# MLP operands made without the norm's factor, and weight sums made in DRAM, in an encoder block on one core

## The chip, the cores and the metric

One of the eight cores of a Trainium2 chip. The metric is the device time of one execution in microseconds (us): the time before is the median of three runs, 1359.18 us (1358.5 to 1359.72). The engines are PE (matrix products), DVE, ACT and POOL (elementwise work), SP (DMA queues), as the profile names them; POOL and ACT have DMA queues too.

## The reference

One layer over 1024 positions of width 1024, all in fp32:

```python
h = rmsnorm(x, norm_mix_g)
z = h @ w_in                                   # split into xc, bg, cg and latents
y_conv = bg * dwconv_centred(cg * xc, conv_w)  # width 512, 3 positions
y_mla = mla_attention(...)                     # 8 heads, from the latents
x = x + concat([y_conv, y_mla]) @ w_o
hf = rmsnorm(x, norm_ffn_g)                    # x * rsqrt(mean(x*x) + eps) * g
a = dwconv_centred(hf @ w_up, ffn_conv_w, ffn_conv_b)
g, u = split(a, 2)                             # 2 x 2816
x = x + (silu(g) * u) @ w_down
gate = sigmoid(rmsnorm(x, ple_norm_g) @ w_ple_gate)
x = x + gate * (p @ w_ple_proj)
return rmsnorm(x, final_norm_g)
```

The norm's factor is one number for each position, a column of the kernel's transposed layout. So it can be multiplied on a product's result as well as on its operand; the gain, one number for each channel, can't.

## The kernel before

Activations lie transposed, channels on the 128 partitions and 1024 positions along the free side, so x is eight tiles (chunks) of 128 x 1024. Each fp32 product is made of three reduced-precision products of high and low parts: an operand is copied to its high part (ACT, `put`, `load_unit`) and the rest is subtracted into the low part (DVE or POOL); `gemm` then issues high by high, high by low and low by high for every 512 columns.

In order of time: latents, conv heads (four of three products each, 60 to 190 us), values, attention (245 to 467; PE, DVE, ACT and POOL share the softmax, and `values(j)` closes each pair of query blocks with POOL's cast and difference, L554 and L555), the attention's half of the output projection (`out_mla`, 474 to 523), the norm of the MLP with the embeds (`embed(d)`, eight products of the layer's input embedding), and the MLP's up projection from 544 to 996, the down projection, the gate and the final norm.

The up projection uses seven products of 512 x 512 blocks in place of eight for each of 22 chunks of the inner width (a `Unit`, steps 1 to 7). The moving operands are four blocks and four sums of blocks of the normed x; the stationary ones are the weights' blocks a11, a12, a22 and sums s1 to s4, which DVE adds for each unit in `stationary` (L654 to L657) before they too are split:

```python
TERMS = {1: ("a11", "b11"), 2: ("a12", "b21"), 3: ("s4", "b22"), 4: ("a22", "t4"),
         5: ("s1", "t1"), 6: ("s2", "t2"), 7: ("s3", "t3")}
```

`up_moving` makes the moving operands: `scaled` multiplies x, in place, by gain and norm factor (L723, 16 halves), `diff` (L726) makes the differences t1 to t4, `put` the high (L734, ACT) and low parts (L726, DVE). The norm's factor comes from two groups of small matmuls that are slipped between those of embeds 2 and 4: sums over the channels (L228) and, after `norm_root`, a broadcast to all partitions (L253). So nothing of `up_moving` can begin before embed 4. The first two units run as a pair, step by step, with embeds 6 and 7 behind step 1; all others run one after another with step 4 one unit late (`run`). Each product's result is read out of PSUM by ACT (a copy) or DVE (L790), goes through a three-point convolution (`conv3`: one ACT step, L261, two DVE steps, L262 and L263) and the silu, and the result is stored to `gud` in DRAM.

What sets the order: the program's order on each engine is made by a scheduler from costs, except where a stretch is put under a manual order, which the text itself then gives; DVE is so from the norm to the end of `up_moving`. A wait holds everything behind it on its engine. Pools of tiles free their memory when the last reader is done, and whatever is placed there waits for that.

Of the kernel before, what the change touches and what calls it, by code (L numbers as in the profile page):

```python
# [33 lines left out]
def tile_block(ctx, tc, xT, pT, wlat, wun, wdn, wuq, wukv, vecs, cst, out):  # L34
# [182 lines left out]
    def norm(sh, sl, dim):  # L217
        n = sh.shape[1] // P
# [185 lines left out]
    for b in range(4):  # L404
# [9 lines left out]
        tt(out=t1, in0=pb, in1=t1, op=ALU.mult)  # L414
# [225 lines left out]
    def stationary(g, u, n, mid, mk, later):  # L640
        lo, hi = slice(0, n), slice(n, 2 * n)
        a = {}

# [10 lines left out]
        tt(out=s14[:, lo], in0=u[:, lo], in1=u[:, hi], op=ALU.add)  # L654
        tt(out=s23[:, lo], in0=s14[:, lo], in1=g[:, lo], op=ALU.subtract)
        tt(out=s14[:, hi], in0=g[:, hi], in1=s23[:, lo], op=ALU.subtract)
        tt(out=s23[:, hi], in0=g[:, lo], in1=u[:, lo], op=ALU.subtract)  # L657
# [17 lines left out]
    class Unit:  # L675
# [3 lines left out]
        def step(self, i):  # L679
# [34 lines left out]
    def up_moving(rs, then):
        sub = ALU.subtract
        bs = [{} for _ in range(4)]
        low = [None]

        def scaled(c, i):
            o = x1[c][:, HALF[i]]
            stt(out=o, in0=o, scalar=vc(V_FFN + c), in1=rs[i], op0=ALU.mult, op1=ALU.mult)  # L723

        def diff(o, p, q):
            tt(out=o, in0=p, in1=q, op=sub)  # L726

        def behind(fn):
            if low[0]:
                low[0]()  # L730
            low[0] = fn

        def put(src, h, z):
            nc.scalar.copy(out=h, in_=src)  # L734
# [391 lines left out]
```

## Time and profile before

| | before |
|---|---|
| median of 3 runs | 1359.18 us |
| profiled execution | 1356.78 us, of which span 1355.0 |
| mean granted clock of PE | 0.989 |
| busy: PE, DVE, ACT, POOL | 1323.1, 1006.1, 597.3, 261.3 us |
| moved by DMA | 117.38 MB, 87 GB/s |
| conv heads | 60 to 190 us |
| attention | 245 to 467 us |
| output projection, embeds, norm | 474 to 544 us |
| up projection: first pair, the 20 others | 544 to 609, 609 to 999 us |

The profile is one execution; its span is the time from the first to the last instruction. In a row of a group stand line, engine, operation, tiles, shapes and count, then busy us, mean ns of one, idle time before them, and who ended it. In a row of a timeline stand start and length in us; idle time before it, with its releaser, is in brackets. A matmul's length runs past the start of the next one, so work of PE is counted from start to start.

### The profile page before, as it was taken

What the parts mean: (1) busy time and instruction counts of PE and PEld (TensorE: products, weight loads), DVE (VectorE), ACT (ScalarE), POOL (GpSimd) and SP (SyncE); (2) the same over time, 40 slices, a digit from 0 to 9 for tenths busy, and PEclk for the clock granted to TensorE, in tenths of its full rate; (3) what the DMA queues carried; (4) which work ended last, traced back from release to release, by engine and by line L of the source; (5) the groups of instructions that cost most, each with busy time, mean ns of one, the idle gap of its engine ahead of it and who ended that gap; (6) DMA issues with size and microseconds to landing.
All of it is one profiled execution on the core that took longest, in us unless ns stands there. A gap on an engine that the chain in (4) does not pass through costs nothing.

```text
span 1355.0 us, 16462 instructions
## 1 busy us (share of the span) xinstructions
PE 1323.1 (98%) x6354; PEld 1087.7 (80%) x6354; DVE 1006.1 (74%) x1336; ACT 597.3 (44%) x839; POOL 261.3 (19%) x222
## 2 busy tenths in 40 slices
PE   9999999999999999879999999999999999999997
PEld 7877788888888887658888888888877888888897
DVE  7478923799999957988887888888665555557786
ACT  5323422788888834543443444344331111125433
POOL 0286452455555510000000000000010000000000
PEclk9999999999999999979999999999999999999998
DMA  6201134200000254203222222222174222121123
GB/s 215 78 31 47 47 133 148 78 1 17 1 17 1 68 212 171 94 16 124 78 78 78 94 78 78 78 94 74 66 292 165 95 94 94 55 78 55 49 83 111
DMA packets 38894, 117.38 MB, mean 87 GB/s; under 512 B 4256, under 2 KB 9632, under 8 KB 38816
## 3 DMA queue, kind: packets, MB, share of 16 engines
q1 hardware_dynamic: 35824, 107.30, 22.7%
q10 hardware_dynamic: 1840, 4.83, 0.9%
q0 software_dynamic: 1152, 4.19, 0.8%
q8 instruction: 50, 0.82, 0.3%
q14 instruction: 28, 0.23, 0.0%
HBM read 88.00 MB, written 28.31 MB: 86 GB/s over the span
## 4 chain that ended last, share of the span: by engine, by line
PE 85%; DVE 9%; issue 2%; POOL 2%; ACT 1%; DMA 0%; POOLq 0%; SPq 0%; ACTq 0%
PE bk L139 56%; PE big L139 9%; PE small L139 4%; PE small L534 4%; PE small L547 2%; PE big L504 2%; PE big L508 2%; PE big L506 2%; PE small L546 2%; DVE tmp L163 1%; DVE xt L726 1%; DVE tmp L263 1%; DVE tmp L262 1%; DVE b L726 1%; DVE rbc L164 1%
## 5 line engine op out<-in xcount | busy, mean ns | idle before, releaser
L139 PE MATMUL bk<-gu,whi 128*128 128x512 f32 x704 | 194.7, 398 | 2.8 <-DVE x L904 2.2
L139 PE MATMUL bk<-b,wm 128*128 128x512 f32 x792 | 192.8, 396 | 1.7 <-DVE b L726 1.4
L139 PEld LDWEIGHTS bk<-b,wm 128*128 128x128 f32 x792 | 148.5, 188 | 38.7 <-DVE b L726 2.5
L139 PEld LDWEIGHTS bk<-gu,whi 128*128 128x128 f32 x704 | 133.0, 189 | 36.0 <-issue 2.6
L904 DVE TENSOR_TENSOR x<-bk,x 128x512 f32<-128x512 f32 x112 | 71.9, 687 | 89.3 <-PE bk L139 88.8
L139 PE MATMUL bk<-xt,wm 128*128 128x512 f32 x528 | 129.3, 399 | 7.6 <-DVE xt L726 5.4
L128 ACT ACTIVATE whi<-wraw 128x1024 fp32r<-128x1024 f32 (+2 forms) x55 | 51.3, 933 | 187.7 <-PE bk L139 135.4
L139 PEld LDWEIGHTS bk<-xt,wm 128*128 128x128 f32 x528 | 100.8, 192 | 32.6 <-DVE xt L726 7.8
L139 PE MATMUL bk<-b,whi 128*128 128x512 f32 x352 | 112.4, 400 | 3.1 <-DVE b L726 3.1
L646 POOL TENSOR_TENSOR wm<-wraw,wm 128x512 fp32r<-128x512 f32 x22 | 28.8, 1311 | 448.9 <-ACT wm L645 448.9
L139 PE MATMUL bk<-gu,wlo 128*128 128x512 f32 x352 | 111.3, 397 | 0.0
L790 DVE TENSOR_TENSOR tmp<-bk,tmp 128x512 f32<-128x512 f32 x110 | 75.6, 687 | 30.6 <-PE bk L139 30.5
L521 POOL TENSOR_SCALAR tmp<-tmp,sm 128x256 f32<-128x256 f32 x64 | 70.2, 1097 | 101.2 <-DVE sm L514 98.5
L261 ACT ACTIVATE tmp<-tmp,vec 128x1024 f32<-128x1024 f32 x44 | 54.5, 1238 | 71.1 <-DVE tmp L790 71.1
L511 DVE TENSOR_REDUCE mx<-big 128x1 f32<-128x1024 f32 x64 | 78.0, 1218 | 10.3 <-PE big L508 9.8
L537 DVE TENSOR_TENSOR ptl<-small,pth 128x512 fp32r<-128x512 f32 x128 | 83.1, 679 | 1.2 <-ACT pth L536 0.9
L139 PEld LDWEIGHTS bk<-b,whi 128*128 128x128 f32 x352 | 66.9, 190 | 20.2 <-DVE b L726 4.2
L262 DVE SCALAR_TENSOR_TENSOR tmp<-tmp,vec 128x1023 f32<-128x1023 f32 x48 | 63.9, 1331 | 21.6 <-ACT tmp L261 19.2
L139 PEld LDWEIGHTS bk<-gu,wlo 128*128 128x128 f32 x352 | 66.4, 189 | 16.0
L536 ACT CAST pth<-small 128x512 fp32r<-128x512 f32 x128 | 69.0, 591 | 19.8 <-PE small L534 17.3
L513 ACT ACTIVATE tmp<-big,mx 128x1024 f32<-128x1024 f32 x64 | 72.1, 1127 | 5.2 <-DVE sm L514 2.6
L139 PE MATMUL big<-hh,whi 128*128 128x512 f32 x224 | 71.0, 397 | 3.3 <-DVE tmp L414 3.1
(291 smaller groups left out, 2793.6 us busy)
## 6 DMA issues: line engine op xcount, KB each, us to landing
wraw<-in_wun_dram SPq DMA_DIRECT2D x73, 512.0 KB, 3.2
gud<-tmp SPq DMA_DIRECT2D x22, 512.0 KB, 2.6
tmp<-gud SPq DMA_DIRECT2D x22, 512.0 KB, 4.3
wraw<-in_wdn_dram SPq DMA_DIRECT2D x24, 384.0 KB, 3.1
tmp<-in_xT_dram SPq DMA_DIRECT2D x15, 512.0 KB, 4.1
x1d<-tmp SPq DMA_DIRECT2D x8, 512.0 KB, 2.8
xt<-x1d SPq DMA_DIRECT2D x8, 512.0 KB, 6.4
x2d<-xt SPq DMA_DIRECT2D x8, 512.0 KB, 2.7
```

What stands on the lines that cost most here:

```text
L128: act(out=wh, in_=raw, func=AF.Copy)
L139: mm(p, w, x[:, s], start=a, stop=z, skip_group_check=more)
L261: act(out=t, in_=src, func=AF.Identity, scale=vc(w + 1), bias=vc(bias))
L262: stt(out=t[:, 1:S], in0=src[:, 0:S - 1], scalar=vc(w), in1=t[:, 1:S], op0=ALU.mult, op1=ALU.add)
L511: nc.vector.tensor_reduce(m, p, AX.X, ALU.max, negate=True)
L513: act(out=e, in_=p, func=AF.Exp, bias=m, accum_out=su)
L521: nc.gpsimd.tensor_scalar(out=e[:, w:S], in0=e[:, w:S], scalar1=su, scalar2=None, op0=ALU.mult)
L534: nc.tensor.transpose(t[:, k, :], e[:, (g * 4 + k) * P:(g * 4 + k) * P + P], ident)
L536: nc.scalar.copy(out=pth[:, ks, qs], in_=t)
L537: tt(out=ptl[:, ks, qs], in0=t, in1=f(pth)[:, ks, qs], op=ALU.subtract)
L790: add = lambda o, p, q: tt(out=o, in0=p, in1=q, op=ALU.add)
L904: tt(out=x1[d][:, s], in0=q, in1=x1[d][:, s], op=ALU.add)
```

## The change

1. *Moving operands without the norm's factor.* `gain(c)` (ACT, in place) multiplies a half of x by the gain alone once its half of x2 has been stored. Operands of chunks 0, 1 and 2 (b11, t1, t3: `put_1`, `put_3`) are made inside the loop of the output projection, from d = 4 on, and the others around the embeds. No `scaled` is left. The norm's factor is copied by ACT from PSUM to `rr`, and DVE multiplies it on the results: two halves of the gate (L858 in place of ACT's copy, L867) and the whole of the other (L871) in each unit. Signs change with it: b22 is negated, and so are the convolution weights of the neighbours.
2. *Weight sums in DRAM.* The up weights come as four block arrays. For each pair of chunks four plain DMAs (DRAM to DRAM, 512 KB) and four that add to their destination make s1 to s4 (`block_sums`, `add_blocks`), all on POOL's queue: 24 in attention, one behind each `values`, for the first three pairs of chunks, and 64 beside the MLP, four in each unit. A unit loads seven blocks of 256 KB instead of two of 512 KB.
3. *Order.* All eight embeds come ahead of the pair's first step (`embed(1)` has the norm's first matmuls in its middle, `embed(5)` its broadcast ahead of it); the pair's convolutions are put off to between its last steps, the third unit's weights are begun there. POOL has a manual order from attention to the MLP's end.
4. *Memory and smaller edits.* x1 lies in halves of 512 columns and is loaded and stored so; b21 and b22 lie where the attention's results did, which is kept up to the MLP's end; in the conv heads ACT copies a head's third product out of PSUM ahead of DVE's multiplication.

```diff
@@ norm @@
-                    tiny.append(lambda t=t, i=i, z=z: mm(p8[0][:, 2 * t:2 * t + 2], z[:, t * P:t * P + P], onesr[:, 0:2], start=i == 0, stop=i == 1))
+                    tiny.append(lambda t=t, i=i, z=z: mm(p8[0][:, 2 * t:2 * t + 2], z[t // 4][:, t % 4 * P:t % 4 * P + P], onesr[:, 0:2], start=i == 0, stop=i == 1))
@@ conv heads @@
-        tt(out=t1, in0=pb, in1=t1, op=ALU.mult)
+        bc = ft()
+        nc.scalar.copy(out=bc, in_=pb)
+        tt(out=t1, in0=bc, in1=t1, op=ALU.mult)
@@ attention @@
+    wsum = [{m: dram.tile([64, 2048], F32, name=f"w{m}_{b}") for m in ("s1", "s2", "s3", "s4")} for b in range(NFF // 2)]
+    dmas = []
+
+    def block_sums(bs):
+        for m, src, op in (("s1", A21, None), ("s2", A11, None), ("s3", A11, None), ("s4", A12, None),
+                           ("s1", A22, ALU.add), ("s3", A21, ALU.add), ("s2", "s1", ALU.add), ("s4", "s2", ALU.add)):
+            for b in bs:
+                dmas.append((wsum[b], m, src, b, op))
+
+    def add_blocks():
+        if dmas:
+            w, m, src, b, op = dmas.pop(0)
+            i = w[src] if isinstance(src, str) else wup[src, 64 * b:64 * b + 64]
+            if op is None:
+                nc.gpsimd.dma_start(out=w[m], in_=i)
+            else:
+                nc.gpsimd.dma_start(out=w[m], in_=i, accum_op=op, max_dma_last_dim=8192)
+
+    block_sums(range(3))
+    pool_order.enter_context(tc.manual_schedule(engines={mybir.EngineType.Pool}))
...
             values(i // 2 - 1)
+            add_blocks()
@@ output projection @@
+    def gain(c):
+        for x in x1[c]:
+            act(out=x, in_=x, func=AF.Copy, scale=vc(V_FFN + c))
...
     for d in range(NC_):
         out_mla(d, [3] if d < 3 else [0, 1, 2, 3])
         if d < 7:
-            for p, s in pieces(accs[d]):
-                tt(out=x1[d][:, s], in0=p, in1=x1[d][:, s], op=ALU.add)
-            square_acc(ss, x1[d], d == 0, nc.vector)
-        nc.sync.dma_start(out=x2d[d], in_=x1[d]) if d < 7 else None
+            q = ss if d == 0 else ft()
+            for p, x, s in zip(accs[d] if isinstance(accs[d], list) else halves(accs[d]), x1[d], HALF):
+                tt(out=x, in0=p, in1=x, op=ALU.add)
+                act(out=q[:, s], in_=x, func=AF.Square)
+                nc.sync.dma_start(out=x2d[d][:, s], in_=x)
+            if d:
+                tt(out=ss, in0=ss, in1=q, op=ALU.add)
+            gain(d)
+        if d in (4, 5, 6):
+            put_1(d - 4)
+            put_3(d - 4)
+            behind(None)
@@ stationary @@
-        tt(out=s14[:, lo], in0=u[:, lo], in1=u[:, hi], op=ALU.add)
-        tt(out=s23[:, lo], in0=s14[:, lo], in1=g[:, lo], op=ALU.subtract)
-        tt(out=s14[:, hi], in0=g[:, hi], in1=s23[:, lo], op=ALU.subtract)
-        tt(out=s23[:, hi], in0=g[:, lo], in1=u[:, lo], op=ALU.subtract)
@@ up_moving @@
-        def scaled(c, i):
-            o = x1[c][:, HALF[i]]
-            stt(out=o, in0=o, scalar=vc(V_FFN + c), in1=rs[i], op0=ALU.mult, op1=ALU.mult)
@@ up_unit @@
-        raws = [load_raw(wun[U_UP + 2 * c + j]) for j in range(2)]
+        load(g[:, T1S], block(wup[A11], c))
+        load(g[:, T2S], block(wup[A12], c))
+        load(u, block(wup[A22], c))
+        for to, m in ((s14[:, T1S], "s1"), (s14[:, T2S], "s4"), (s23[:, T1S], "s2"), (s23[:, T2S], "s3")):
+            load(to, block(wsum[c // 2][m], c % 2))
...
             elif i == 2:
-                nc.scalar.copy(out=g1, in_=p)
+                tt(out=g1, in0=p, in1=rr[:, T1S], op=ALU.mult)
...
+                if len(half) == 2:
+                    tt(out=g2, in0=g2, in1=rr[:, T2S], op=ALU.mult)
...
-                add(u1, p, u1)
+                diff(u1, u1, p)
+                tt(out=au, in0=au, in1=rr, op=ALU.mult)
@@ the pair @@
-    for i in (1, 5, 2, 3, 6, 7, 4):
-        for unit in pair:
-            unit.step(i)
-        if i == 1:
-            embed(6)
-            embed(7)
+    embed(4)
+    norm_second()
+    embed(5)
+    for i in range(2):
+        nc.scalar.copy(out=rr[:, HALF[i]], in_=rs[i])
+    embed(6)
+    embed(7)
+    for i in (1, 5):
+        for unit in (u0, u1):
+            unit.step(i)
...
+    for b in range(3, NFF // 2):
+        block_sums([b])
+    run(u2)
```

How the order on an engine moves is seen at three places. DVE in the output projection, around the evacuation of d = 4 and 5 (xt is x1, big PSUM, tmp_4650 and tmp_4755 the sum of squares, b1 an operand's low part; L625 and L726 add the projection's result to x1). Before:

```order
L280 TENSOR_TENSOR tmp_4650<-tmp_4650,tmp_4709 128x1024
L625 TENSOR_TENSOR xt_4545<-big_4725,xt_4545 128x1024
L654 TENSOR_TENSOR s14_4873<-wraw_4867 128x512
L657 TENSOR_TENSOR s23_4874<-wraw_4865,wraw_4867 128x512
L655 TENSOR_TENSOR s23_4874<-s14_4873,wraw_4865 128x512
L280 TENSOR_TENSOR tmp_4650<-tmp_4650,tmp_4751 128x1024
L656 TENSOR_TENSOR s14_4873<-wraw_4865,s23_4874 128x512
L625 TENSOR_TENSOR xt_4546<-big_4761,xt_4546 128x1024
```

After:

```order
L726 TENSOR_TENSOR xt_4642<-big_4849,xt_4642 128x512
L726 TENSOR_TENSOR xt_4638<-big_4849,xt_4638 128x512
L730 TENSOR_TENSOR tmp_4755<-tmp_4755,tmp_4874 128x1024
L680 TENSOR_TENSOR xt_4631<-xt_4631,xt_4638 128x512
L680 TENSOR_TENSOR b1_4890<-xt_4630,b1_4889 128x512
L726 TENSOR_TENSOR xt_4643<-big_4904,xt_4643 128x512
L726 TENSOR_TENSOR xt_4639<-big_4904,xt_4639 128x512
L134 TENSOR_TENSOR wlo_4962<-wraw_4959,whi_4961 128x1024
L680 TENSOR_TENSOR b1_4894<-xt_4631,b1_4893 128x512
L680 TENSOR_TENSOR b1_4940<-xt_4632,b1_4939 128x512
```

Operand rows (L680) stand where the weight sums of unit 0 stood. POOL in attention (L521, now L530, scales a part of the softmax; L554 and L555, now L563 and L564, close a pair of blocks). Before:

```order
L521 TENSOR_SCALAR tmp_2061<-tmp_2061,sm_2059 128x256
L554 CAST ymh0_1308<-yt_2099 64x256
L555 TENSOR_TENSOR yml0_1312<-yt_2099,ymh0_1308 64x256
L521 TENSOR_SCALAR tmp_2122<-tmp_2122,sm_2120 128x256
L521 TENSOR_SCALAR tmp_2159<-tmp_2159,sm_2157 128x256
```

After:

```order
L530 TENSOR_SCALAR tmp_2119<-tmp_2119,sm_2117 128x256
L563 CAST ymh0_1317<-yt_2157 64x256
L564 TENSOR_TENSOR yml0_1321<-yt_2157,ymh0_1317 64x256
L603 DMA ws2_0_1731<-in_wup_dram 16x8192
L530 TENSOR_SCALAR tmp_2181<-tmp_2181,sm_2179 128x256
L530 TENSOR_SCALAR tmp_2218<-tmp_2218,sm_2216 128x256
```

A DMA now stands between the difference and the next scaling. DVE at the end of the up projection (gu is the down projection's operand, L268 and now L275 its low part; L262, L263 and now L269, L270 convolve). Before:

```order
L790 TENSOR_TENSOR tmp_8016<-bk_8065,tmp_8016 128x512
L268 TENSOR_TENSOR gu_8163<-tmp_8160,gu_8162 128x1024
L262 SCALAR_TENSOR_TENSOR tmp_8118<-tmp_8016,vec_71,tmp_8118 128x1023
L790 TENSOR_TENSOR tmp_8017<-bk_8051,tmp_8017 128x512
L268 TENSOR_TENSOR gu_8169<-tmp_8166,gu_8168 128x1024
L263 SCALAR_TENSOR_TENSOR tmp_8118<-tmp_8016,vec_71,tmp_8118 128x1023
L262 SCALAR_TENSOR_TENSOR tmp_8136<-tmp_8017,vec_71,tmp_8136 128x1023
L268 TENSOR_TENSOR gu_8175<-tmp_8172,gu_8174 128x1024
```

After:

```order
L867 TENSOR_TENSOR tmp_8278<-tmp_8278,rr_4618 128x512
L680 TENSOR_TENSOR tmp_8279<-tmp_8279,bk_8314 128x512
L269 SCALAR_TENSOR_TENSOR tmp_8382<-tmp_8278,vec_71,tmp_8382 128x1023
L871 TENSOR_TENSOR tmp_8279<-tmp_8279,rr_4618 128x1024
L275 TENSOR_TENSOR gu_8430<-tmp_8427,gu_8429 128x1024
L270 SCALAR_TENSOR_TENSOR tmp_8382<-tmp_8278,vec_71,tmp_8382 128x1023
L275 TENSOR_TENSOR gu_8436<-tmp_8433,gu_8435 128x1024
L269 SCALAR_TENSOR_TENSOR tmp_8401<-tmp_8279,vec_71,tmp_8401 128x1023
L270 SCALAR_TENSOR_TENSOR tmp_8401<-tmp_8279,vec_71,tmp_8401 128x1023
L275 TENSOR_TENSOR gu_8442<-tmp_8439,gu_8441 128x1024
```

The multiplications by the norm (L867, L871) stand ahead of the first low part, and all four convolution steps ahead of the third.

More of the change, by code (lines that the diff above doesn't have):

```diff
@@ L620, in tile_block, with behind, diff, put @@
     dve_order = ExitStack()
+    low = [None]
+    bs = [{} for _ in range(4)]
+    y1, y2 = x1[0:4], x1[4:8]
+    def behind(fn):
+        if low[0]:
+            low[0]()
+        low[0] = fn
+    def diff(o, p, q):
+        tt(out=o, in0=p, in1=q, op=ALU.subtract)
+    def put(src, h, z, sign=1.0):
+        if sign > 0:
+            nc.scalar.copy(out=h, in_=src)
+            behind(lambda: diff(z, src, f(h)))
+        else:
+            act(out=h, in_=src, func=AF.Copy, scale=sign)
+            behind(lambda: stt(out=z, in0=src, scalar=sign, in1=f(h), op0=ALU.mult, op1=ALU.subtract))
+        return h, z
+    def gain(c):
+        for x in x1[c]:
+            act(out=x, in_=x, func=AF.Copy, scale=vc(V_FFN + c))
+    def put_1(k, then=lambda: behind(None)):
+        own = b1 if k < 3 else bt
+        bs[k]["b11"] = put(y1[k][0], own(), own())
+        then()
+        diff(y1[k][0], y1[k][1], y1[k][0])
+        bs[k]["t1"] = put(y1[k][0], own(), own())
+    def put_3(k):
+        diff(y1[k][1], y1[k][1], y2[k][1])
+        bs[k]["t3"] = put(y1[k][1], b1(), b1())
+    def put_b21(k):
+        bs[k]["b21"] = put(y2[k][0], b2s[k][0][:, T1S], b2s[k][1][:, T1S])
+    def put_b22(k):
+        bs[k]["b22"] = put(y2[k][1], b2s[k][0][:, T2S], b2s[k][1][:, T2S], -1.0)
+    def put_t2(k):
+        diff(y2[k][1], y2[k][1], y1[k][0])
+        bs[k]["t2"] = put(y2[k][1], bt(), bt())
+        diff(y2[k][0], y2[k][0], y2[k][1])
+    def put_t4(k):
+        own = bt if k < 2 else b1
+        bs[k]["t4"] = put(y2[k][0], own(), own())
     for d in range(NC_):
@@ L779, in embed @@
             gemm(acc, w[0][:, c], w[1][:, c], ph[k][0], ph[k][1], k == 0, k == 1)
+            if k == 0 and between:
+                between()
         t = ft()
@@ new lines, in finish, with gate, up @@
+        def finish(fn):
+            if post is None:
+                fn()
+            else:
+                post.append(fn)
+        def gate():
+            tpool[0] = tmpb
+            t = conv3(ag, V_FW + 6 * c, V_FB + 2 * c)
+            act(out=t, in_=t, func=AF.Silu)
+            out_.append(t)
+        def up():
+            tpool[0] = tmpb
+            t = conv3(au, V_FW + 6 * c + 3, V_FB + 2 * c + 1)
+            tt(out=t, in0=out_[0], in1=t, op=ALU.mult)
+            nc.sync.dma_start(out=gud[c], in_=t)
@@ new lines, in up_unit @@
+        return Unit(a, bs, read)
+    post = [], []
+    u0 = up_unit(0, None, post[0])
+    weights = []
+    dve_order.enter_context(tc.manual_schedule(engines={mybir.EngineType.DVE}))
+    sq, sh = ft(), halves(ft(FR))
+    for p, x, s in zip(accs[7], x1[7], HALF):
+        tt(out=x, in0=p, in1=x, op=ALU.add)
+        act(out=sq[:, s], in_=x, func=AF.Square)
+        nc.sync.dma_start(out=x2d[7][:, s], in_=x)
+    gain(7)
+    for k in range(2):
+        put_b21(k)
+    for h, z, s in zip(sh, sl, HALF):
@@ L837, in tile_block @@
     norm_first, norm_root, norm_second, rs = norm(sh, sl, D)
+    embed(0)
     for j in range(2):
         embed_weights(j)
[L840 to L858 removed]
+    put_1(3, lambda: put_b21(2))
+    embed(1, norm_first)
+    norm_root()
+    put_b21(3)
+    for k in range(4):
+        put_b22(k)
+    embed(2)
+    embed(3)
+    u1 = up_unit(1, weights, post[1])
+    put_3(3)
+    behind(None)
+    weights.pop(0)()
+    weights.pop(0)()
+    for k in range(4):
+        put_t2(k)
+    for k in (0, 3, 1, 2):
+        put_t4(k)
+    behind(None)
+    embed(4)
[8 more added lines that the diff above has]
+            unit.step(i)
+    weights.pop(0)()
+    weights.pop(0)()
+    for unit in (u0, u1):
+        unit.step(2)
+    u2 = up_unit(2, weights)
+    weights.pop(0)()
+    for i in (3, 6):
+        for unit in (u0, u1):
+            unit.step(i)
+    weights.pop(0)()
+    u0.step(7)
+    u1.step(7)
+    post[0].pop(0)()
+    u0.step(4)
+    weights.pop(0)()
+    weights.pop(0)()
+    post[1].pop(0)()
+    u1.step(4)
+    dve_order.close()
+    post[0].pop(0)()
+    post[1].pop(0)()
+    for b in range(3, NFF // 2):
+        block_sums([b])
+    run(u2)
+    for c in range(3, NFF):
         run(up_unit(c))
     run_last()
+    pool_order.close()
     tmpb_done()
```

187 lines of the change are left out of this document (66 added, 121 removed).

## The prediction

> **What bounds the kernel now.** First the page's first two parts: which engine is full, and where it isn't. In the second each digit is a slice of 33.9 us; slices 16 and 17 are where PE and its granted clock dip.
>
> ```profile
> PE 1323.1 (98%) x6354; PEld 1087.7 (80%) x6354; DVE 1006.1 (74%) x1336; ACT 597.3 (44%) x839; POOL 261.3 (19%) x222
> PE   9999999999999999879999999999999999999997
> PEclk9999999999999999979999999999999999999998
> ```
>
> PE is nearly always busy, so only what PE waits for, or does at a low clock, can be won. Next the table by stretches, cut finely around the dip (columns: length, then busy us and instructions of PE, PEld, DVE, ACT, POOL; granted clock, DMA share, GB/s).
>
> ```profile
> 245.00:467.00 222.00, 220.45 (x1435) 194.28 (x1434) 202.84 (x340) 182.95 (x326) 118.95 (x135) 1.00 0.05 18
> 485.00:505.00 20.00, 20.00 (x87) 16.10 (x86) 14.71 (x14) 8.81 (x10) 1.14 (x2) 1.00 0.59 211
> 555.00:565.00 10.00, 7.88 (x30) 4.97 (x28) 9.97 (x15) 4.94 (x7) 0.00 (x0) 1.00 0.25 98
> 565.00:575.00 10.00, 7.28 (x24) 5.51 (x25) 9.69 (x13) 5.43 (x8) 0.00 (x0) 0.83 0.00 0
> 575.00:585.00 10.00, 6.91 (x26) 4.74 (x24) 9.69 (x15) 4.72 (x8) 0.00 (x0) 0.86 0.00 0
> 585.00:595.00 10.00, 5.95 (x11) 3.44 (x12) 8.94 (x14) 3.84 (x6) 0.00 (x0) 0.50 0.15 52
> 607.00:700.00 93.00, 93.00 (x403) 75.36 (x402) 78.24 (x83) 38.73 (x44) 8.04 (x6) 1.00 0.26 97
> 997.00:1020.00 23.00, 20.25 (x84) 15.59 (x83) 17.46 (x18) 10.09 (x10) 4.43 (x8) 0.98 0.96 371
> ```
>
> From 555 to 595 DVE is the full engine (38.3 of 40 us) and PE gets 28.0, part of it at clocks of 0.50 to 0.86; the steady MLP (607 to 700) is PE alone. What PE waits for from 480 to 625 (us in all, times, longest):
>
> ```profile
> PE bk L139 <- DVE xt L726: 5.4, 4, 2.9
> PE bk L139 <- DVE b L726: 4.5, 4, 2.1
> PE bk L139 <- ACT xt L734: 1.8, 1, 1.8
> ```
>
> L726 and L734 make the MLP's moving operands (differences and low parts, high parts). The timeline of PE bounds the stretch: where the embeds resume, the first matmul of the pair of units, its last wait and the first matmul behind the pair; the last line is the chain of waits, in which PE runs unbroken from there.
>
> ```profile
> 523.99 0.96 PE L139 MATMUL bk<-tmp,whi 128*128 128x512 f32 x3 [0.91 <-DVE xt L824]
> 543.98 0.63 PE L139 MATMUL bk<-b,whi 128*128 128x512 f32 x2
> 606.44 3.03 PE L139 MATMUL bk<-xt,wm 128*128 128x512 f32 x12 [0.42 <-DVE tmp L790]
> 609.31 0.63 PE L139 MATMUL bk<-b,whi 128*128 128x512 f32 x2
> 606.44 389.66 PE bk L139 x1680
> ```
>
> A matmul of 512 columns costs 389.66/1680 = 0.232 us from start to start. Between 543.98 and 609.31 stand 168 matmuls of the pair (2 units, 7 products, 4 chunks, 3 each) and 24 of embeds 6 and 7: 192 x 0.232 = 44.5 us in 65.3. So 20.8 us are lost here, more than the named waits show, because matmuls run at the lower clock too.
>
> **Part 1: operands without the norm.** DVE's groups by shape from 485 to 620, and from its timeline eight halves in a row, which start every 4.87/8 = 0.61 us:
>
> ```profile
> L723 DVE SCALAR_TENSOR_TENSOR xt<-xt,vec,bk 128x512 f32<-128x512 f32 x16 | 11.5, 742 | 1.8 <-PE bk L253 1.8
> L726 DVE TENSOR_TENSOR xt<-xt 128x512 f32<-128x512 f32 x16 | 10.8, 688 | 0.1
> L726 DVE TENSOR_TENSOR b<-xt,b 128x512 fp32r<-128x512 f32 x12 | 8.2, 686 | 0.6 <-ACT b L734 0.5
> L726 DVE TENSOR_TENSOR xt<-xt 128x512 fp32r<-128x512 f32 x8 | 5.3, 689 | 0.0
> L726 DVE TENSOR_TENSOR b<-xt,b 128x1024 fp32r<-128x1024 f32 x4 | 4.8, 1217 | 0.0
> L654 DVE TENSOR_TENSOR s<-wraw 128x512 f32<-128x512 f32 x5 | 4.4, 874 | 0.0
> L656 DVE TENSOR_TENSOR s<-wraw,s 128x512 f32<-128x512 f32 x4 | 3.3, 833 | 0.0
> L655 DVE TENSOR_TENSOR s<-s,wraw 128x512 f32<-128x512 f32 x4 | 2.7, 684 | 0.0
> L657 DVE TENSOR_TENSOR s<-wraw 128x512 f32<-128x512 f32 x4 | 2.7, 684 | 0.0
> 1017.77 4.87 DVE L904 TENSOR_TENSOR x<-bk,x 128x512 f32<-128x512 f32 x8
> ```
>
> Sixteen scalings (11.5 us) leave DVE, and the other operand work (29.1 us for L726) no longer stands behind the norm's broadcast: with the first three chunk pairs it begins in the output projection, where DVE was busy 14.7 of 20 us. The weight sums of the pair (L654 to L657, 13.1 us) leave DVE too. What comes in per unit is a multiplication of a gate half instead of ACT's copy, one more half and one of 1024: at 688 and 1217 ns 2.6 us of DVE, against four sums of 0.68 to 0.87, 3.1 us, taken off. In steady state DVE stays where it was, at 78 of 93 us beside a full PE: 0.
>
> From 486 on DVE must now hold, counted from the order's rows up to the norm's splits, 38 halves at 0.61 and 14 of 1024 (six sums of squares, eight low parts of weights) at 1.2: 40 us, to 526. It is full but hardly overfull, and the evacuations of PSUM stand between the operand rows, so they come in time. The rest up to t2 and t4, some 45 rows of the same sizes, ends near 557. PE reaches the pair at 523.99 + 8 embeds x 12 x 0.232 = 22.3 + 3.3 for the norm's small matmuls (20.0 us were used by six embeds and them, less 16.7) = 549.6; t2 is needed by the fifth step (product 6), after 4 steps of 2 units of 12 x 0.232 = 2.8 us, 22 us, at 572. b11 and t1 are made by then. Estimate: PE unbroken but for about 1 us, where embed 1 now runs the norm's first matmuls and waits for the splits. Gain 20.8 - 1.0 = **19.8 us**; bounds 12 (first rival) and 20.8.
>
> The gains now run on ACT in place, so each waits until that half of x2 is stored; ACT was busy 8.8 of 20 us there. That delays operands, not evacuations; cover is DVE's 15 us lead on t2.
>
> **Part 2: sums in DRAM.** No row shows a copy from DRAM to DRAM or one that adds. Nearest are a plain transfer (page, KB each, us to landing) and POOL's issue of seven:
>
> ```profile
> tmp<-gud SPq DMA_DIRECT2D x22, 512.0 KB, 4.3
> 997.80 3.89 POOL L891 DMA_DIRECT2D x<-x2d  x7 [33.25 <-PE bk L139]
> ```
>
> Issue: 3.89/7 = 0.56 us with DVE busy beside it. In attention 24 are issued, one in a slot of POOL's order, where it waits anyway:
>
> ```profile
> 303.96 0.75 POOL L555 TENSOR_TENSOR yml<-yt,ymh 64x256 fp32r<-64x256 f32 x1
> 307.25 1.19 POOL L521 TENSOR_SCALAR tmp<-tmp,sm 128x256 f32<-128x256 f32 x1 [2.54 <-DVE sm L514]
> 309.55 1.04 PE L534 MATMUL small<-ident,tmp 128*128 128x128 f32 x8
> ```
>
> An issue of 0.56 fits into 2.54 and costs nothing; with the 1.1 us from L521's end (308.44) to its transposes, up to 3.6 us is hidden. If that cover is gone every microsecond is paid 24 times; bounds 0 and, at an issue of twice the gap (5.1), 24 x 1.5 = 36 us. I take 0, by the row. [...]
>
> Beside the MLP 64 are issued, four per unit; the accumulates of a pair are a chain of three after its copies and are ordered two to three units (39 to 58 us) before their use. At 4.3 us each the chain takes 17; bounds 0 cost up to this lead, and I take 0. Loads per unit grow from 1.0 to 1.75 MB, the sums move some 2 MB per unit more: the DMA share goes from 0.26 (97 GB/s, 1.9 MB a unit of 19.5 us) to about 0.26 x 4.65/1.9 = 0.64. Free.
>
> **Part 3: smaller edits.** The conv heads: ACT copies the product out of PSUM before DVE multiplies.
>
> ```profile
> 60.00:190.00 130.00, 126.88 (x542) 101.22 (x541) 97.91 (x78) 41.76 (x49) 77.58 (x30) 1.00 0.17 57
> PE big L139 <- DVE tmp L414: 3.1, 3, 1.6
> L536 ACT CAST pth<-small 128x512 fp32r<-128x512 f32 x128 | 69.0, 591 | 19.8 <-PE small L534 17.3
> ```
>
> ACT is busy 42 of 130 us there, and two such halves take 1.2 us instead of waiting for DVE's queue: gain **2.6** (0 to 3.1). At the MLP's end (a group of the page, then two waits of PE's timeline):
>
> ```profile
> L262 DVE SCALAR_TENSOR_TENSOR tmp<-tmp,vec 128x1023 f32<-128x1023 f32 x48 | 63.9, 1331 | 21.6 <-ACT tmp L261 19.2
> 1001.26 0.72 PE L139 MATMUL bk<-gu,whi 128*128 128x512 f32 x2 [0.56 <-DVE gu L268]
> 1018.61 2.11 PE L139 MATMUL bk<-gu,whi 128*128 128x512 f32 x4 [2.15 <-DVE x L904]
> ```
>
> Now the low parts of the down projection's first two blocks stand on DVE behind two multiplications by the norm (0.7 and 1.2) and two convolution steps (1.3 each), and loads of the next blocks wait on SP for the memory of b21 and b22, which PE reads in the last products. The first group comes 0.7 + 1.2 + 2.6 = 4.5 us later than now; of that the 2.15 us of the wait on L904, and a little of the low clock behind it, are absorbed, since its evacuations now stand ahead of the next low part. Loss **2.0** (0 to 5). The output projection's weight casts and first evacuations, behind unit 0's two sums in DVE's order: loss **0.5** (0 to 2).
>
> Sum against the profiled execution (1356.78, span 1355.0): -19.8 - 2.6 + 2.0 + 0.5 = -19.9, so 1336.9; the median of the runs is 2.4 above it: 1359.2 - 19.9 = **1339.3 us**.
>
> **Rivals.** *Preparation stays bound by DVE.* For it: DVE is full up to 526, and behind ACT's gains, which wait for stores. Against: 15 us lead on t2; it decides where t2 comes after 572. If each of the 38 halves waited 0.6 us, as long as it takes itself, t2 would come at 557 + 23 = 580 and PE lose 8: 1347. *The loss at the MLP's end is not absorbed,* 5 instead of 2, with the clock dropping: 1343 to 1344. *POOL's issues hold the softmax* (slower). Decides where an issue in attention takes over 3.6 us; it turns the sign where it takes 3.6 + 19.9/24 = 4.4 us. At 5.1: 1339.3 + 36 = 1375. For it: POOL's gaps are short and DVE is busy 202.84 of 222 us there; against: 0.56 in the row. *Sums come late* (slower, or no change): an accumulate of over 13 to 19 us (39 to 58 us by three) makes every later pair wait; eight pairs at 5 us each give 1379. Against: 4.3. For: no row shows an accumulate.
>
> [...]
>
> **Numbers.** Forecast 0.66; DVE-bound preparation 0.15; the end's loss 0.07; POOL's issues 0.07; late sums 0.05. The range 1333 to 1352 takes in the bounds of the gains (20.8 + 3.1 and no loss: 1335, less 2 for a clock better than now) and the second case's 1347 with 5 at the end; it leaves out the slower cases and a part of the edge, 0.2. A change under 0.2% (2.7 us) can't be told from none. Faster 0.86 (the first three, less 0.02), same 0.04, slower 0.10.
>
> **What would show it.** Right: PE's row from 555 to 600 full at clock 1.00, no L723, steady units 19.5 us apart with the first after the pair near 589; no wait of PE on the multiplication in conv heads; POOL's issues about 0.6 us; waits of the sums' loads only off PE's path. Wrong: transposes waiting for L530 (the new number of L521) in attention, PE waiting on the low parts of sums in the MLP, or on the first gate product of the down projection for more than 5 us.

## The result, and the profile after

The change made the kernel slower: 1372.82 us (median of four, 1371.62 to 1375.79) against 1358.84 of the kernel before beside it, a ratio of 1.0117 with a 95% interval of 1.0105 to 1.0129. The forecast was 1339.3 (1333 to 1352). The profiled execution has a span of 1374.0 us, 19.0 over the 1355.0 of before. It was the slowest of the four, so the profiles differ by more than the medians (14.0 us); a difference of a microsecond or two between stages of single executions says little by itself.

The page's first two parts of the changed kernel: PE's share fell by a point, the dip at slices 16 and 17 (counted from 0) is gone, and new ones stand at slices 8, 10 and 12 (275 to 447 us, attention) and at 29 (996 to 1030, the end of the up projection).

```profile
PE 1330.5 (97%) x6354; PEld 1095.9 (80%) x6354; DVE 1012.6 (74%) x1309; ACT 605.3 (44%) x850; POOL 322.1 (23%) x310
PE   9999999989897999999999999999979999999998
PEclk9999999999999999999999999999989999999998
```

The waits of PE over the whole span (us in all, times, longest) name both places:

```profile
PE small L144 <- POOL wlo L134: 16.9, 3, 6.4
PE bk L144 <- ACT gu L274: 5.5, 2, 4.6
PE bk L144 <- DVE gu L275: 2.9, 2, 2.6
PE big L144 <- POOL wlo L134: 2.1, 2, 1.9
PE big L144 <- DVE wlo L134: 1.6, 1, 1.6
PE big L144 <- ACT whi L133: 1.0, 1, 1.0
```

The operand waits of before (L726 and L734) are no longer there, and no wait on a weight sum is. From the table by stretches of the changed kernel (columns as before: length, busy us and instructions of PE, PEld, DVE, ACT and POOL, granted clock, DMA share, GB/s): attention with a mean clock of 0.96, two stretches where the old dip stood, the steady MLP, and its end.

```profile
245.00:467.00 222.00, 202.70 (x1271) 177.18 (x1271) 180.93 (x303) 162.91 (x290) 125.80 (x144) 0.96 0.28 69
555.00:565.00 10.00, 9.20 (x34) 7.80 (x35) 9.45 (x24) 5.88 (x12) 1.28 (x1) 0.66 0.64 232
575.00:585.00 10.00, 10.00 (x44) 8.06 (x43) 9.34 (x15) 6.17 (x12) 0.00 (x0) 1.00 0.74 264
607.00:700.00 93.00, 93.00 (x403) 75.34 (x402) 83.30 (x83) 40.19 (x41) 19.89 (x25) 1.00 0.79 245
997.00:1020.00 23.00, 19.16 (x75) 14.32 (x74) 16.04 (x17) 6.27 (x6) 3.74 (x7) 0.93 0.67 236
```

Four marks divide a span: the first and the last score product of attention, the last product of the up projection, the end. The lengths between them in all runs (us, one profiled execution each; what the edits are is told below):

| kernel | to the first score | attention's scores | from there to the up projection's end | from there to the end | span |
|---|---|---|---|---|---|
| before | 236.6 | 231.3 | 530.8 | 356.3 | 1355.0 |
| changed | 238.4 | 255.1 | 515.9 | 364.6 | 1374.0 |
| e1, weights early | 236.4 | 231.7 | 517.7 | 364.6 | 1350.4 |
| e2, before with POOL's order | 236.5 | 254.0 | 529.7 | 356.3 | 1376.5 |
| e3, changed, POOL's order from behind attention | 285.9 | 231.3 | 517.2 | 363.9 | 1398.3 |
| e5, before with the copy in the conv heads | 234.8 | 231.3 | 532.3 | 355.0 | 1353.5 |
| e6, e1 with the norm later | 236.8 | 231.7 | 515.4 | 364.4 | 1348.3 |
| e8, e1 with weights ahead | 238.3 | 231.7 | 515.0 | 365.1 | 1350.1 |
| e7, e1 with x2 behind | 237.0 | 231.0 | 515.7 | 354.7 | 1338.4 |
| e9, all three | 235.1 | 231.1 | 514.7 | 354.6 | 1335.5 |
| e10, before with x2 behind | 236.6 | 230.8 | 531.2 | 355.3 | 1353.9 |
| e11, e9 with the broadcast later | 236.5 | 231.2 | 507.7 | 355.9 | 1331.3 |

So the changed kernel lost 23.8 us in attention and 8.3 at the end, won 14.9 in the preparation of the operands, and began 1.8 later.

**Attention, read closely.** POOL's timeline of before and of the changed kernel, at the first of the three waits:

```profile
288.78 0.40 POOL L554 CAST ymh<-yt 64x256 fp32r<-64x256 f32 x1 [0.69 <-DVE yt L553]
289.26 0.73 POOL L555 TENSOR_TENSOR yml<-yt,ymh 64x256 fp32r<-64x256 f32 x1
290.16 1.30 POOL L268 TENSOR_TENSOR qtl<-tmp,qth 128x512 fp32r<-128x512 f32 x1 [0.17 <-ACT qth L267]
```

```profile
290.64 0.40 POOL L563 CAST ymh<-yt 64x256 fp32r<-64x256 f32 x1 [0.69 <-DVE yt L562]
291.12 0.72 POOL L564 TENSOR_TENSOR yml<-yt,ymh 64x256 fp32r<-64x256 f32 x1
291.79 0.57 POOL L603 DMA_DIRECT2D ws<-in_wup_dram  x1
292.44 1.25 POOL L134 TENSOR_TENSOR wlo<-wraw,whi 128x512 fp32r<-128x512 f32 x1
297.35 1.28 POOL L275 TENSOR_TENSOR qtl<-tmp,qth 128x512 fp32r<-128x512 f32 x1 [3.66 <-ACT qth L274]
```

And PE there, in the changed kernel:

```profile
287.58 0.28 PE L557 MATMUL small<-pth,v 128*128 128x256 f32 x1
288.22 0.40 PE L144 MATMUL small<-ql,whi 128*128 128x512 f32 x1
293.74 0.80 PE L144 MATMUL small<-qh,wlo 128*128 128x512 f32 x1 [5.12 <-POOL wlo L134]
```

PE starts the last matmul of `values` at 287.58 and goes on to the next query heads' products, which need the low part of their weights (`wlo`, L134). That row stands on POOL behind the cast that waits for this very `values`, its difference and the DMA. So PE waits for a chain that its own last product began: until 290.64 for the copy on ACT and the sum on DVE (L561, L562), then 0.40 + 0.72 + 0.57 + 1.25 on POOL. In before, where a scheduler made POOL's order, the same row stood far earlier, 43 us ahead of its first use at 286.59:

```profile
243.96 1.29 POOL L129 TENSOR_TENSOR wlo<-wraw,whi 128x512 fp32r<-128x512 f32 x1 [2.01 <-ACT whi L128]
```

The other two stood at 265.97 and 324.55, for uses at 345.19 and 404.30, and none of the three waits existed. The DMA is 0.57 of the 5.1 us.

### The profile page after: what moved, and what is told of

The parts are those of the page before. It is cut to its first block, busy times and chain, and to the rows that moved or that the text cites. A ratio compares the mean times of both kernels' runs of the same rounds, so it can differ in the third digit from the quotient of the medians.

```text
span 1374.0 us, 16816 instructions
## 1 busy us (share of the span) xinstructions
PE 1330.5 (97%) x6354; PEld 1095.9 (80%) x6354; DVE 1012.6 (74%) x1309; ACT 605.3 (44%) x850; POOL 322.1 (23%) x310
## 4 chain that ended last, share of the span: by engine, by line
PE 88%; DVE 5%; POOL 2%; ACT 2%; DMA 2%; issue 1%; POOLq 0%; DVEq 0%; ACTq 0%
PE bk L144 57%; PE big L144 13%; PE small L144 4%; PE small L543 3%; PE big L513 2%; PE big L515 2%; PE big L517 2%; PE small L556 2%; PE small L555 2%; DVE mx L520 1%; DMA tmp<-gud 1%; DVE ptl L546 1%; POOL wlo L134 1%; DMA x2d<-xt 1%; DVE tmp L168 0%
## 5 line engine op out<-in xcount | busy, mean ns | idle before, releaser
L144 PE MATMUL bk<-b,wm 128*128 128x512 f32 x594 | 149.2, 396 | 0.0
L144 PEld LDWEIGHTS bk<-b,wm 128*128 128x128 f32 x594 | 111.6, 188 | 26.5
L133 ACT ACTIVATE whi<-wraw 128x1024 fp32r<-128x1024 f32 (+2 forms) x55 | 51.3, 932 | 180.5 <-PE bk L144 136.6
L144 PE MATMUL bk<-xt,wm 128*128 128x512 f32 x462 | 116.0, 390 | 0.0
L680 DVE TENSOR_TENSOR tmp<-tmp,bk 128x512 f32<-128x512 f32 x110 | 75.2, 685 | 40.5 <-PE bk L144 40.5
L144 PEld LDWEIGHTS bk<-xt,wm 128*128 128x128 f32 x462 | 86.8, 188 | 19.2
L757 POOL TENSOR_TENSOR wm<-wraw,wm 128x512 fp32r<-128x512 f32 x22 | 29.7, 1352 | 285.0 <-ACT wm L756 285.0
L530 POOL TENSOR_SCALAR tmp<-tmp,sm 128x256 f32<-128x256 f32 x64 | 71.5, 1117 | 99.5 <-DVE sm L523 96.0
L268 ACT ACTIVATE tmp<-tmp,vec 128x1024 f32<-128x1024 f32 x44 | 54.8, 1244 | 58.7 <-DVE tmp L871 31.6
L269 DVE SCALAR_TENSOR_TENSOR tmp<-tmp,vec 128x1023 f32<-128x1023 f32 x48 | 65.0, 1355 | 18.7 <-ACT tmp L268 16.2
L756 ACT CAST wm<-s 128x1024 fp32r<-128x1024 f32 x44 | 46.0, 1047 | 69.7 <-PE bk L144 66.9
L144 PE MATMUL big<-hh,wlo 128*128 128x512 f32 x224 | 71.5, 400 | 1.9 <-POOL wlo L134 1.9
```

Of the source, the lines that this page charges most:

```text
L133: act(out=wh, in_=raw, func=AF.Copy)
L144: mm(p, w, x[:, s], start=a, stop=z, skip_group_check=more)
L268: act(out=t, in_=src, func=AF.Identity, scale=vc(w + 1), bias=vc(bias))
L269: stt(out=t[:, 1:S], in0=src[:, 0:S - 1], scalar=vc(w), in1=t[:, 1:S], op0=ALU.mult, op1=ALU.add)
L530: nc.gpsimd.tensor_scalar(out=e[:, w:S], in0=e[:, w:S], scalar1=su, scalar2=None, op0=ALU.mult)
L680: tt(out=o, in0=p, in1=q, op=ALU.subtract)
```

## The experiments

**e1, the heads' weights early (four executions).** The load and the split move from behind the `values` of a head's third block to ahead of the `values` of its first; all else is the change.

```diff
-        if h % 2 == 0 and n == 0:
-            uq[0] = load_unit(wuq[h // 2], 512)
+        if h == 0 and n == 0:
+            uq[0] = load_unit(wuq[0], 512)
...
         transposes(i)
+        if i % 8 == 0 and h % 2 == 1 and h < H - 1:
+            uq[0] = load_unit(wuq[(h + 1) // 2], 512)
         if i % 2 == 0 and i >= 2:
```

> The change with one edit: a query head's weights are loaded and split at the head's first block (i % 8 = 0), ahead of its values and DMA, instead of at the third; POOL's order stays manual and all 24 DMAs stay in attention. Order theory (the low part of the weights stands behind a pair's close on POOL because the order is manual): PE's three waits on POOL wlo L134 (16.9 us) go, attention shrinks by 17 to 24 us, the time falls to 1349 to 1356. Issue theory (the DMA issues hold POOL and with it the softmax): nothing moves, 1370 to 1374. Traffic theory (the transfers slow loads and stores): nothing moves either.

Measured: 1351.68 us against 1356.89, ratio 0.9953 (0.9935 to 0.997): the change with one statement moved is faster than before. The rows of the score products in before, the changed kernel and e1 (ns of one, then first and last start):

```profile
L504 PE MATMUL big<-kth,qth x128: 389/397/484, 236.6 to 467.9; 128*128 128x512 f32 x128
```

```profile
L513 PE MATMUL big<-kth,qth x128: 389/398/628, 238.4 to 493.5; 128*128 128x512 f32 x128
```

```profile
L513 PE MATMUL big<-kth,qth x128: 389/398/484, 236.4 to 468.1; 128*128 128x512 f32 x128
```

With all 24 DMAs still in attention it takes 231.7 us, 0.4 more than before (231.0 to 231.7 in all later variants that keep them). That is the whole price of the issues and of their traffic; the issue and the traffic theories fall.

**e2, POOL's manual order alone, in the kernel before (one profiled execution).**

```diff
+    pool_order = ExitStack()
+    pool_order.enter_context(tc.manual_schedule(engines={mybir.EngineType.Pool}))
     for i in range(NT):
...
+    pool_order.close()
     at_done()
```

> The kernel before with one edit: POOL's order is manual in attention, no DMA is added. Order theory: three waits of PE on POOL wlo L129 of 4 to 6 us appear, attention grows by 16 to 24 us, the span is 1371 to 1379. Issue and traffic theories: no change, the span stays at 1355.

Measured: span 1376.5, attention 254.0 us, 22.7 longer, without a single DMA added. The three waits are there:

```profile
PE small L139 <- POOL wlo L129: 14.8, 3, 5.6
```

The waits are 14.8 us and the loss 22.7. The rows of attention from its first to its last score product, of before and of e2, tell where the rest is:

```profile
236.60:467.90 231.30, 229.75 (x1477) 202.06 (x1476) 207.85 (x347) 187.13 (x332) 121.57 (x137) 1.00 0.06 21
236.50:490.50 254.00, 237.36 (x1477) 207.33 (x1476) 208.40 (x347) 186.95 (x332) 123.64 (x137) 0.96 0.06 20
```

PE's idle time grows from 1.6 to 16.6 us, which is the waits, and the same 1477 matmuls take 7.6 us longer at a mean clock of 0.96: 0.68, 0.72 and 0.66 in the 10 us from 290, 350 and 420, around the waits. So a third of the loss is the low clock behind the waits.

**e3, the manual order only from behind attention (one profiled execution).**

```diff
     pool_order = ExitStack()
-    pool_order.enter_context(tc.manual_schedule(engines={mybir.EngineType.Pool}))
     for i in range(NT):
...
+    pool_order.enter_context(tc.manual_schedule(engines={mybir.EngineType.Pool}))
     at_done()
```

> The change, but POOL's manual order begins behind attention, so that the scheduler places the weights' low parts and the 24 DMAs there. Order theory: as the first run, attention within 2 us of before's, the span 1349 to 1357. Issue theory: attention stays 20 us or more longer. If the scheduler places DMAs ahead of what the softmax needs, a part of it stays.

Measured: span 1398.3, so my number was wrong, though attention fell back to 231.3 us (scores from 285.9 to 517.2). The scheduler moved all 24 DMAs, which wait for nothing but one another, to the head of POOL's queue (issued from 1.2 to 53.2 us), where they hold up the loads of x: e3's chain of waits stands on one of these for 37.45 us from 21.86, that of before for 3.79 from 1.64. The first 60 us by the table of stretches, in before and in e3:

```profile
0.00:60.00 60.00, 57.92 (x237) 45.52 (x238) 36.15 (x65) 25.37 (x29) 5.18 (x6) 1.00 0.47 157
0.00:60.00 60.00, 19.22 (x52) 13.25 (x52) 10.00 (x27) 5.31 (x6) 15.63 (x28) 0.76 0.99 271
```

PE works 19 of 60 us at a DMA share of 0.99, against 58 at 0.47. A fixed order for POOL is there for a reason; it was incomplete, not superfluous.

**e5, the copy in the conv heads alone, in the kernel before (one profiled execution).**

```diff
-        tt(out=t1, in0=pb, in1=t1, op=ALU.mult)
+        bc = ft()
+        nc.scalar.copy(out=bc, in_=pb)
+        tt(out=t1, in0=bc, in1=t1, op=ALU.mult)
```

> The kernel before with ACT's copy in the conv heads alone. My prediction: the three waits on DVE L414 (3.1 us) go and 2.6 us are won, the span is 1352 to 1353. Rival, from the trace of the changed kernel: a wait on POOL wlo L129 of 1.9 us takes the place of the second, so 0.3 to 1.2 us are won, the span is 1354 to 1355.

Measured: span 1353.5, scores from 234.8 instead of 236.6, so 1.8 us, between the two expectations. The waits on L414 are gone and one on POOL is in their place:

```profile
PE big L139 <- POOL wlo L129: 2.1, 2, 1.8
```

Before, e2 and e10, which lack the copy, have the first score at 236.5 or 236.6. The stages behind it came out 1.5 us longer and 1.3 shorter than before's, with unchanged code, so the span says less than this mark. In the changed kernel and its variants other than e3 the first score comes between 235.1 and 238.4, so there this gain is not seen apart from what else moves in these 236 us.

**e6 and e8, the two stalls of the preparation (one profiled execution each, on e1).** e6 moves the norm's first matmuls from embed 1 to embed 2; e8 loads and splits the output projection's weights for d = 4 and 6 ahead of d = 3 and 5.

```diff
-    embed(1, norm_first)
-    norm_root()
+    embed(1)
     put_b21(3)
+    embed(2, norm_first)
+    norm_root()
     for k in range(4):
         put_b22(k)
-    embed(2)
```

```diff
-        if d % 2 == 0 and ks[0] == 0:
+        if d % 2 == 0 and ks[0] == 0 and d // 2 not in ws:
...
     for d in range(NC_):
+        if d in (3, 5):
+            ws[d // 2 + 1] = load_unit(wun[U_OM + d // 2 + 1])
         out_mla(d, [3] if d < 3 else [0, 1, 2, 3])
```

> The first run's kernel (early weights) with the norm's first matmuls in embed 2 instead of embed 1. Theory: embed 1 meets the splits of the sum of squares too early, PE waits 1.8 us there and then runs at half clock until about 545, 4 us lost in all; so the two waits on DVE L909 and L910 go and the pair's first matmul comes 3 to 4 us earlier: span 1346 to 1348. Rival: the low clock comes from the output projection's stall at 511 to 514 alone, and 0 to 2 us are won: 1348 to 1350.

> The first run's kernel with the output projection's weights for d = 4 and 6 loaded and split ahead of d = 3 and 5. Theory: at 511 and 514 PE waits because ACT's cast of these weights stands behind gains and squares (ACT is never idle from 498 to 511); moved ahead, the waits of 1.2 and 1.6 us and about 1 us of low clock go: span 1346 to 1348. Rival: the gains are late instead and PE waits the same time elsewhere in the stage: 1350.

Measured (spans): e6 1348.3, within the rival's 1348 to 1350. From attention to the up projection's end it is 2.3 us shorter than e1: the waits in embed 1 went, but 2.0 us on the norm's root (DVE nyh L248) came. e8 1350.1: the waits on the output projection's weights went and that stage is 2.7 us shorter, while the start of this execution was 1.9 later and the waits in embed 1 grew from 1.8 to 2.5. e7 has neither edit and yet 515.7 in this stage, 2.0 under e1, so from one execution each neither is settled to better than 2 us; each stall mostly moved on to the next late thing.

**e7, the loads of x2 behind the third block (one profiled execution, on e1).** POOL copies one column of the down projection's third block before it issues the eight loads of x2 (and its order stays manual up to there).

```diff
-    pool_order.close()
...
         if g == 0:
+            nc.gpsimd.tensor_copy(out=const.tile([P, 1], F32, name="third"), in_=y[:, 0:1])
             for d in range(NC_):
                 nc.gpsimd.dma_start(out=x1[d], in_=x2d[d])
+            pool_order.close()
```

> The first run's kernel; at the end of the up projection POOL copies one column of the down projection's third block before it issues the eight loads of x2, so these begin when the third block has landed. Contention theory: the third block's load takes 10.9 us because 4 MB of x2 stand in the queues ahead of it; alone it takes 3 to 4, the wait of 3.9 us on ACT gu L274 falls under 1 us, and the span is 1344 to 1347. Order theory (the late low part on DVE is all there is): the wait stays, 1350. Rival cost: x2 comes too late for L1021 and PE waits there instead, 1349 to 1354.

Measured: span 1338.4, 12.0 us under e1, 9.9 of them behind the up projection's end. In the changed kernel the chain of waits and PE's timeline read:

```profile
1013.59 10.85 DMA tmp<-gud
```

```profile
1010.30 0.73 PE L144 MATMUL bk<-gu,whi 128*128 128x512 f32 x2 [0.93 <-ACT gu L274]
1013.62 0.73 PE L144 MATMUL bk<-gu,whi 128*128 128x512 f32 x2 [2.58 <-DVE gu L275]
1025.56 2.48 PE L144 MATMUL bk<-gu,whi 128*128 128x512 f32 x4 [4.61 <-ACT gu L274]
```

The third block's buffer comes free when DVE has made the first low part, at 1013.57. In before that was 997.95, 0.7 us ahead of the up projection's end (998.65); here it is 4.2 behind (1009.4). By then POOL has issued seven loads of x2 (1007.37 to 1011.55), and the block's load, issued on SP's queue, takes 10.9 us behind them. In before it was issued together with them (997.97, POOL from 997.80), and ACT's cast of the block began at 1001.90. In e7 the loads of x2 start at 992.91, when the block has landed (issued at 987.91, cast from 992.54), and the third wait is gone:

```profile
984.63 0.73 PE L144 MATMUL bk<-gu,whi 128*128 128x512 f32 x2 [0.93 <-ACT gu L274]
987.94 0.94 PE L144 MATMUL bk<-gu,whi 128*128 128x512 f32 x2 [2.58 <-DVE gu L275]
```

It won over twice the wait of 3.9 us that stood in e1. In the first 40 us behind the up projection's end PE is idle for 7.9 us in e1 and for 3.5 in e7, at mean clocks of 0.83 and 0.96, so the waits and the clock make about half of the gain each. Parts of it in the table of stretches, of e1 and then of e7:

```profile
990.00:995.00 5.00, 4.97 (x12) 3.88 (x13) 4.78 (x4) 1.17 (x2) 0.00 (x0) 0.50 1.00 365
1005.00:1010.00 5.00, 5.00 (x14) 3.91 (x13) 4.76 (x6) 1.36 (x2) 0.00 (x0) 0.56 0.96 326
```

```profile
990.00:995.00 5.00, 5.00 (x20) 3.80 (x19) 4.07 (x5) 2.33 (x3) 2.25 (x5) 0.83 0.90 306
1005.00:1010.00 5.00, 5.00 (x23) 4.02 (x22) 3.43 (x6) 0.85 (x1) 0.00 (x0) 1.00 1.03 422
```

**e9, all three edits of e6, e8 and e7 on e1 (four executions), and e10, the edit of e7 alone in the kernel before (ten executions; POOL's order is manual for the copy and the loads only).**

> The three edits together on the first run's kernel. If the three theories hold and add up, 3.5 + 3 + 4 us below it: 1340 to 1343 in time, ratio to the kernel before 0.986 to 0.989. If each stall only moves to the next late thing, 1347 to 1351.

> The kernel before with the last edit alone: POOL copies a column of the down projection's third block ahead of the loads of x2. If the 10 us that this edit won behind the early weights were the change's own loss given back, the kernel before wins only what its two waits there cost (0.56 and 2.15 us and a little low clock): span 1352 to 1354. If they were independent of the change, it wins 8 us or more: 1347 or less. It can lose where x2 comes late for L904: 1356 to 1360.

Measured: e9 1337.58 against 1356.91, ratio 0.9862 (0.9846 to 0.9879). The sum of my three sizes gave 1340 to 1343; e7 alone was larger than I had it, the other two edits shortened their stage by only 1.0 us beyond it (515.7 to 514.7), and a wait of 4.0 us on the norm's root had come up:

```profile
PE bk L260 <- DVE nyh L248: 4.0, 1, 4.0
```

e10: 1355.66 against 1356.8, ratio 0.9988 (0.9979 to 0.9998), 1.1 us. Its two waits (0.56 and 2.15 us) are still there, so where the 1.1 us come from is not shown. So of the 9.9 us that the edit won on e1 nearly all was the change's own loss given back (8.3 by the table); the kernel before had little to win here.

**e11, the broadcast two embeds later (four executions).** e9 with the norm's broadcast moved from embed 5 to embed 7.

```diff
-    norm_second()
     embed(5)
-    for i in range(2):
-        nc.scalar.copy(out=rr[:, HALF[i]], in_=rs[i])
     embed(6)
+    norm_second()
     embed(7)
+    for i in range(2):
+        nc.scalar.copy(out=rr[:, HALF[i]], in_=rs[i])
```

> The kernel with all three edits, with the norm's broadcast moved from embed 5 to embed 7. Theory: PE's wait of 4.0 us on DVE nyh L248 is there because the norm's root ends on DVE at 539 and PE reaches the broadcast at 535; two embeds (5.6 us) cover it, and the half clock behind it goes too: 3 to 5 us, time 1333 to 1335. Rival: DVE, which waits for the broadcast with one low part (b1 lies in the identity's memory), is held longer and the operands t2 and t4 come late: 1337 to 1341.

Measured: 1333.04 against 1356.8, ratio 0.982 (0.9805 to 0.9835), the fastest of all. The rival fell: PE has no wait on DVE from 480 us to the up projection's end, so t2 and t4 were not late. The table of stretches of e11, around the embeds, and from attention to the up projection's end, where before had clocks down to 0.50:

```profile
525.00:535.00 10.00, 10.00 (x54) 8.52 (x53) 7.96 (x14) 8.72 (x17) 0.00 (x0) 1.00 0.68 223
535.00:545.00 10.00, 10.00 (x53) 8.46 (x52) 7.64 (x24) 6.13 (x12) 1.40 (x1) 1.00 0.84 303
545.00:555.00 10.00, 10.00 (x46) 8.11 (x45) 9.94 (x15) 6.23 (x12) 0.00 (x0) 1.00 0.49 159
468.00:975.00 507.00, 506.65 (x2229) 411.38 (x2227) 418.90 (x455) 227.44 (x276) 76.14 (x94) 1.00 0.67 204
```

## Why the prediction was wrong

The step that failed is in part 2: "In attention 24 are issued, one in a slot of POOL's order, where it waits anyway", with a term of 0 for attention. The price of an issue was about right (0.57 us plain, 0.82 to 0.86 with an addition, and 0.4 us in all by e1). But the change put POOL's whole order into the program's hands, and I weighed only the rows that were added to it, not those that were moved: three splits of weights went from far ahead of their use to behind the step that PE had just fed. This was to be read in the program's text, which is POOL's order there: `q_head`, with its `load_unit`, stands behind `values` and `add_blocks`. It costs 22.7 us by itself (e2), more than the forecast gain of 19.9. My slower rival had POOL hold PE up in attention, but named the issue's length as what decides, which no run bears out; the sign that I gave for it, transposes waiting for L530, did not come either (they wait 1.3 us in all, for DVE, as in before). That its 1375 lies near the measured 1372.8 is luck.

Point by point. The preparation: forecast 19.8 (bounds 12 to 20.8); the changed kernel won 14.9, e1 13.1. The mechanism was right, operands no longer bound the stage. The term was mis-sized. "About 1 us" in embed 1 was two waits of 1.2 us in all, at the norm's first matmuls, and 4.8 us with the low clock behind them (0.66 from 555 to 565; the embeds took from 550.3 to 580.6, 25.6 of it by my count):

```profile
555.35 0.27 PE L233 MATMUL bk<-onesr,tmp 128*128 128x2 f32 x1 [0.69 <-DVE tmp L907]
556.07 0.27 PE L233 MATMUL bk<-onesr,xt 128*128 128x2 f32 x1 [0.46 <-DVE xt L908]
```

And the output projection's "0.5" was waits of 2.6 us (L133 and L134), where before has 1.3, because ACT's cast of weights stood behind the gains and squares. With both out of the way and the broadcast later (e11) the stage is 23.1 us shorter than before, more than my upper bound, as stalls that before has also go.

The up projection with its sums: forecast 0, and it held. The chain of waits of e1 has PE unbroken through it at 435.18/1876 = 0.232 us a matmul, as in before:

```profile
550.62 435.18 PE bk L144 x1876
```

A sum's DMA landed in 7.1 us (from the weights, plain and added) and 7.7 us (from another sum), over my 4.3, and the DMA share was 0.79, over my 0.64; the lead of two units covers both.

The end of the up projection: forecast a loss of 2.0 (0 to 5), measured 8.3. That the first low parts stand 4.5 us later was right (4.9 by the buffer's release). "Are absorbed" was wrong: the third block's load hangs on the first low part, and is now issued behind the loads of x2, which do not move with it. This and the low clock behind it are what e7 gives back.

The conv heads: forecast 2.6, 1.8 in e5, with a wait on POOL in place of DVE's. The start: the changed kernel's profiled execution has the first score 1.8 us later, after its first products ran slowly (0.43 us from start to start until 11.0 us, 0.23 in e1 from 7.7 on); e1 has the same code there and is 0.2 earlier than before, so that is no cost of the change.

The clock: the three waits in attention, of 5.12, 5.40 and 6.35 us, were followed by mean clocks of 0.58, 0.71 and 0.53 in the 5 us from 293.7, 359.9 and 426.4, where 280 to 290, 340 to 354 and 405 to 420 had 1.00. In the preparation no wait of that length stands, and still waits of 0.69 and 0.46 us, one right behind the other, went with a mean clock of 0.66 from 555 to 565 in the changed kernel. But not every short wait does it: in the output projection the changed kernel waits 0.99 and 1.62 us and keeps a clock of 1.00 from 536 to 550, while in e1 the same two waits (1.19 and 1.64 us) are followed by matmuls 0.43 us from start to start until 517.3 and a mean clock of 0.86 from 515 to 525. What decides is not shown. Of the rivals one had a dropping clock, the forecast none; a low clock behind each stall belonged into it, as a possible surcharge.

## What to carry to other kernels

When an engine's order is taken from a scheduler and written down, any row of that engine can move, not only the added ones: go through the rows that another engine waits for, and ask of each what now stands ahead of it. A split of weights written at its use, behind a step that depends on the consumer's own last work, makes a loop through several engines; written ahead of the `values` before that, it cost 0.4 us at most here. And a load whose buffer comes free later can be late by more than that, by whatever has been put ahead of it in the meantime: here a buffer that came free 4.9 us later cost 8.3.

## What the runs showed that I had not expected

DVE's multiplication of 1024 by the norm (L871), two operands in SBUF, took 1.21 to 1.23 us in four units and 2.17 to 2.21 in seventeen, and the latter where POOL had begun a subtraction 0.2 us ahead of it (once 1.85, with POOL 0.5 us ahead); where DVE was first, POOL's took longer (1.83 us against 1.29 to 1.33). Both timelines of the changed kernel, two pairs:

```profile
642.77 1.23 DVE L871 TENSOR_TENSOR tmp<-tmp,rr 128x1024 f32<-128x1024 f32 x1
643.32 1.83 POOL L757 TENSOR_TENSOR wm<-wraw,wm 128x512 fp32r<-128x512 f32 x1 [0.24 <-ACT wm L756]
662.05 1.29 POOL L757 TENSOR_TENSOR wm<-wraw,wm 128x512 fp32r<-128x512 f32 x1 [14.95 <-ACT wm L756]
662.25 2.17 DVE L871 TENSOR_TENSOR tmp<-tmp,rr 128x1024 f32<-128x1024 f32 x1
```

In the second pair DVE ends 1.08 us after POOL's 663.34, nearly its own full length of 1.21; in the first POOL ends 1.15 us after DVE's 644.00, of its own 1.29. So in these rows they run one after the other; why is not shown. It costs DVE about 1 us in most units, which PE does not wait for here: the chain of waits has PE unbroken for 434.43 us from 574.96. POOL's DMA issues in attention showed nothing like it: in the changed kernel they took 0.57 us plain (once 0.72) and 0.82 to 0.86 with an addition, with DVE busy 180.9 of 222 us.
